# A one-layer encoder step: source order for the first stage on two engines, an earlier identity, and a shared rotation of eight PSUM banks

## The chip, the cores and the metric

The kernel runs on one core of one Trainium2 chip. A core has five engines with queues of their own: TensorE (PE in the profile, its weight loads PEld), VectorE (DVE), ScalarE (ACT), GpSimd (POOL) and SyncE (SP), which here only issues DMAs. Each engine serves its queue in order and waits on semaphores. The metric is the device time of one execution in microseconds, lower is better.

## The reference

One layer of a streaming encoder, for 256 rows of a new stream and 8 streams of 16 rows each: 384 rows in all, which share the weights.

```python
h    = rmsnorm(x, norm_mix_g)
proj = h @ w_in                      # conv gate pair | q | k | v | forget logits | gate A | gate B
u    = glu_in[..., :D_CONV] * sigmoid(glu_in[..., D_CONV:])
z    = layernorm(causal_dwconv(concat([conv_buf, u]), conv_dw_w, conv_dw_b), conv_ln_g, conv_ln_b)
a_out = (z * sigmoid(z)) @ conv_pw_out
q, k = rmsnorm(q, q_norm_g), rmsnorm(k, k_norm_g)
logf = log_sigmoid(f_logit + b_forget)
b_out = attn_fn(q, k, v, logf) @ w_att_out
x    = x + (sigmoid(gate_a) * a_out + sigmoid(gate_b) * b_out) @ w_out
h2   = rmsnorm(x, norm_ffn_g)
up   = h2 @ w_up                     # gate half | value half, each 5632 wide
gc   = causal_dwconv(concat([ffn_buf, g_half]), ffn_dw_w, ffn_dw_b)
x    = x + (silu(gc) * u_half) @ w_down
```

The model is 2048 wide, with 8 heads of 128. All is float32, and besides the rows the new k, v, logf and the two convolution states are returned.

## The kernel before, in words

Every product is made in three float32r matmuls. A weight block `raw` (256 rows by up to 512 columns, two k steps) is loaded from HBM, ScalarE casts it to `hi` (L145), and VectorE subtracts for `lo` (L146). The activations are kept as such pairs too, 16 chunks of 128 features. A unit is one k step of one job: three row tiles (or four feature tiles) times hi x hi, hi x lo, lo x hi, nine matmuls on L244 to L246, or twelve on L239 to L241 where the weights are the stationary side. A job accumulates 8 to 16 k steps in three PSUM banks (four on L239 to L241) and is then evacuated.

The order of the work is set in several ways. TensorE's order is the source's for the whole kernel (`pe_order`, a manual schedule). ScalarE, VectorE and SyncE are ordered by hand only in the opening part, up to the second weight block; after that a planner orders their instructions by readiness in its own model and by a priority. The priority is the place in the source, moved ahead by an offset: 150 for loads and splits (`SPLIT_AHEAD`), 400 for evacuations (`EVAC_AHEAD`). `queued` adds an edge to the engine's newest queued instruction, which fixes the order of the two and waits for nothing. `tc.keep_in_program_order` adds such an edge to the instruction before in the source. Before, `queued` is used on SP alone, for loads.

`plan` lists the weight blocks in the order of use, and `ahead(n)` loads and splits blocks until n are ready. In the first stage (the v columns, 344 wide, two jobs interleaved and then a third) n is 2, later 3. There are three raw, three hi and three lo tiles. `gemm` walks the units, and after each calls `tick`, which advances side work: generators that yield once per unit.

The side work of the first stage is `first_norm`: per chunk c of x, `x_chunk(c)` transposes three row tiles on TensorE (L285), copies them to hi, times the norm's gain, on ScalarE (L288) and makes lo on VectorE (L289). Chunks 2 and 3 are transposed after the third and fourth unit and used in the fifth and sixth; the block used there is the third. For each four chunks ScalarE makes three squares with a sum (L400). The sums give the row scale `rs1`, through a root on ScalarE and a Newton step on VectorE (`newton_rsqrt`, L110 to L116), which the evacuations of v need (`tok_evac`, L428).

The identity for transposes and for warm-up matmuls (L308) is made on POOL by a memset and a select. POOL's queue also issues the loads of eight small vectors (L348 to L352).

PSUM has eight banks in two pools: five `acc`, which the jobs take, and three `misc`, for transposes and the small products of attention. Only the second of two interleaved jobs takes its third bank from misc. The evacuation of k and q makes the squares for the head norm within the loop over the three banks (L431 to L434).

Attention is side work in the four convolution-gate jobs (L239 to L241): per head six steps at set units, with the loads of cached k and v on SP. The taps of the depthwise convolution (L722) run on VectorE beside it and after it. Behind attention come the gate jobs, the attention and convolution outputs (`ao_evac` L828, `pw_evac` L843 and L844, `mix_chunk` L850), the output product, and the feed-forward part, which ends in `down` jobs (L1018).

Of the kernel before, what the change touches and what calls it, by code (L numbers as in the profile page):

```python
# [8 lines left out]
F32 = mybir.dt.float32  # L9
F32R = mybir.dt.float32r  # L10
AF = mybir.ActivationFunctionType
ALU = mybir.AluOpType
# [3 lines left out]
P = 128  # L16
DM = 2048
NT = 384
NTT = 3
# [11 lines left out]
LN_LAG = 0  # L31
SQ_LAG = 1
MIX_FIRST, MIX_EVERY = 2, 2
SPLIT_AHEAD, EVAC_AHEAD = 150, 400

R_FFN, R_DWB, R_LNG, R_LNB, R_FDB, R_QG, R_N = 0, 16, 24, 32, 40, 84, 85
WARM, FILL = 5, 2
# [3 lines left out]
def hybrid_step(  # L41
# [34 lines left out]
    def f(ap):  # L76
        return ap.bitcast(F32)
# [39 lines left out]

    def rsqrt(m, shape, p, tag):
        s = p.tile(shape, F32, tag=tag + "s", name=tag + "s")
        r = p.tile(shape, F32, tag=tag + "r", name=tag + "r")  # L120
        newton_rsqrt(r[:], s[:], m)
        return r
# [19 lines left out]
        return [wp.tile([P, 2, 512], F32R, tag=tag, bufs=3, name=tag) for tag in ("hi", "lo")]  # L142

    def split_rows(hi, lo, raw, o, k):
        nc.scalar.copy(hi[:, k, :o], raw[:, k, :o])  # L145
        tt(lo[:, k, :o], raw[:, k, :o], f(hi[:, k, :o]), op=ALU.subtract)  # L146

    def split(raw, o):
        hi, lo = split_tiles()
# [56 lines left out]
    def grouped(tiles):  # L206
        def get(k):
            t = tiles[k // 4]
            return t[:, 0, k % 4, :], t[:, 1, k % 4, :]
        return get  # L210
# [7 lines left out]
        for g in sides:  # L218
            next(g, None)

    def gemm(jobs, sides=()):
        for js in jobs:
            js = js if isinstance(js, tuple) else (js,)
            for j in js:
                nb = 4 if j["kind"] == "A" else NTT
                j["ps"] = [(misc_tile if j is not js[0] and i == 2 else acc_tile)() for i in range(nb)]
            for j, k in [(j, k + i) for k in range(0, js[0]["nk"], 2) for j in js for i in range(2)]:
                nb, n, nk, ps = len(j["ps"]), j["n"], j["nk"], j["ps"]
                kk = k % 2
                if kk == 0:  # L230
                    ahead(2 if len(plan) > v_last + 3 else 3)
                    hi, lo = ready.pop(0)
                ah, al = j["act"](k)
                st, sp = k == 0, k == nk - 1
                for m in range(nb):
                    s = slice(m * P, (m + 1) * P)
                    if j["kind"] == "A":
                        o = ps[m][:, :NT]
                        mm(o, hi[:, kk, s], ah, start=st, stop=False)  # L239
                        mm(o, hi[:, kk, s], al, start=False, stop=False)  # L240
                        mm(o, lo[:, kk, s], ah, start=False, stop=sp)  # L241
                    else:
                        o = ps[m][:, :n]
                        mm(o, ah[:, s], hi[:, kk, :n], start=st, stop=False)  # L244
                        mm(o, ah[:, s], lo[:, kk, :n], start=False, stop=False)  # L245
                        mm(o, al[:, s], hi[:, kk, :n], start=False, stop=sp)  # L246
# [35 lines left out]
    def x_chunk(c):  # L282
        ps = misc_tile()
        for t in range(NTT):
            tr(ps[:, t * P:(t + 1) * P], xs[c // 4][:, t, c % 4 * P:(c % 4 + 1) * P], ident[:])  # L285
        g = gm[:, c:c + 1]
        hi, lo = hT[c // 4][:, 0, c % 4, :], hT[c // 4][:, 1, c % 4, :]
        nc.scalar.activation(hi, ps[:, :NT], AF.Identity, scale=g)  # L288
        stt(lo, ps[:, :NT], g, f(hi), op0=ALU.mult, op1=ALU.subtract)  # L289

    pe_order = tc.manual_schedule(engines={ENG.PE})
    pe_order.__enter__()
# [52 lines left out]
    rows = [(norm_ffn_g, R_FFN, 16), (conv_dw_b, R_DWB, 8), (conv_ln_g, R_LNG, 8),  # L345
            (conv_ln_b, R_LNB, 8), (ffn_dw_b, R_FDB, 44), (q_norm_g, R_QG, 1)]
    for v, r, n in rows:
        nc.gpsimd.dma_start(vrow[r:r + n, :], v[0].rearrange("(c p) -> c p", p=P))  # L348
    kg = p_qkv.tile([P, P], F32, name="kg")
    nc.gpsimd.dma_start(kg[:], k_norm_g[0].partition_broadcast(P))  # L350
    bf = p_qkv.tile([P, H], F32, name="bf")
    nc.gpsimd.dma_start(bf[:], b_forget[0].partition_broadcast(P))  # L352
# [35 lines left out]
    def first_norm():  # L388
        for c in range(2, 16, 2):
            if c == 2:  # L390
                yield
            yield
            x_chunk(c)
            yield
            x_chunk(c + 1)
            if c % 4 == 2:
                for t in range(NTT):
                    n = c // 4
                    tc.keep_in_program_order(
                        nc.scalar.activation(junk[:], xs[n][:, t, :], AF.Square, accum_out=ssx[:, t, n:n + 1]))  # L400
            yield
            if c > 2:
                yield
        mt = p_x0.tile([P, NTT], F32, name="mt")
        nc.vector.tensor_reduce(mt[:], ssx[:], axis=mybir.AxisListType.X, op=ALU.add)
        ts(mt[:], mt[:], 1.0 / DM, EPS, op0=ALU.mult, op1=ALU.add)
        r = rsqrt(mt[:], [P, NTT], p_x0, "r1")
        nc.vector.tensor_copy(rs1[:], r[:])
# [11 lines left out]
    lg = p_qkv.tile([P, NTT, H], F32, name="lg")  # L420
    ssq = p_qkv.tile([P, 2, NTT, H], F32, name="ssq")

    def tok_evac(dst, c0, n, sq=None, shared=True):
        def ev(t, ps):
            if shared and t % 2:
                ts(dst[:, t, c0:c0 + n], ps[:, :n], rs1[:, t:t + 1], None, op0=ALU.mult)
            else:
                nc.scalar.activation(dst[:, t, c0:c0 + n], ps[:, :n], AF.Identity, scale=rs1[:, t:t + 1])  # L428
            if sq is not None:
                for i in range(n // P):  # L430
                    jk = p_qkv.tile([P, P], F32, tag="jk", bufs=2, name="jk")  # L431
                    h = c0 // P + i
                    nc.scalar.activation(jk[:], dst[:, t, h * P:(h + 1) * P], AF.Square,
                                         accum_out=ssq[:, sq, t, h:h + 1])  # L434
        return ev

    ha = grouped(hT)
# [76 lines left out]
    gemm([job("B", 16, ha, tok_evac(kt, 512 * i, 512, 0)) for i in range(2)], [bias_rows()])  # L514
    close_b()
    rk = head_rsqrt(0)
    for t in range(NTT):
# [6 lines left out]
    gemm([job("B", 16, ha, tok_evac(qt, 512 * i, 512, 1)) for i in range(2)])  # L524
    rq = head_rsqrt(1)
    for t in range(NTT):
        q3 = qt[:, t, :].rearrange("p (h d) -> p h d", h=H)
# [123 lines left out]
    def attention():  # L651
        at = {}
        for d in heads:
            for off, step in ((0, head_past_keys), (2, head_operands), (4, head_scores), (9, head_probs),
                              (11, head_out), (13, head_last)):
                at[ATT_FIRST + 6 * d["h"] + off] = step, d
        for t in range(max(at) + 1):
            if t in at:
                step, d = at[t]
                step(d)  # L660
                if step is head_out and d["h"] + 2 < H:
                    load_v(d["h"] + 2)
            yield
# [104 lines left out]
    def sig_evac(dst, n):  # L768
        def ev(t, ps):
            nc.scalar.activation(cols_of(dst, t, n), ps[:], AF.Sigmoid, scale=rs1[:, t:t + 1])  # L770
        return ev
# [59 lines left out]
    def ao_job(n):  # L831
        return job("B", 8, grouped(aHL), ao_evac(n))

    gemm([ao_job(n) for _, n in AO_PW[:2]], [ln_steps])
    drain(ln_steps)


# [27 lines left out]
    def pw_done(n):  # L865
        def done():
# [5 lines left out]
        return done  # L872

    gemm([ao_job(n) if what == "ao" else job("B", 8, grouped(zt), pw_evac(n), done=pw_done(n))
          for what, n in AO_PW[2:]])


    res = {}
# [50 lines left out]
        r2 = rsqrt(m2[:], [P, NTT], p_f, "r2")  # L929
        nc.vector.tensor_copy(rs2[:], r2[:])  # L930

    gemm([job("B", 16, grouped(mix), wo_evac(n), done=wo_done(n)) for n in range(4)])


    p_f, y, xg, rs2, close_f, close_r = (res[k] for k in ("f", "y", "xg", "rs2", "close_f", "close_r"))
# [88 lines left out]
        return [job("B", 4 * len(gs), grouped(tiles), evac(n)) for n in range(4)]  # L1024

    for what, g in FFN_PLAN:
        gemm(up_jobs(g) if what == "up" else down_jobs(g, g[-1] == 10))

    pe_order.__exit__(None, None, None)
    close_f()  # L1030
# [42 lines left out]
```

## Time and profile before

| | |
|---|---|
| median of 3 runs | 2005.61 us (2002.94 to 2005.78) |
| profiled execution | 2005.83 us |
| its span, first to last instruction | 2003.9 us |
| instructions | 24493 |
| busy: DVE, ACT, POOL | 1272.2, 742.1, 87.2 us |
| HBM traffic over the span | 137 GB/s |

In the profile a row of the timeline is start, duration, engine, line, operation, output<-inputs, shapes, count, and in brackets the idle time before it with what ended it. Matmuls overlap in the pipeline, so the distance between starts is the pace and the duration is longer. The granted clock is TensorE's, as a share of full speed. A busy share close to 1 for TensorE says only that it always had a matmul in flight.

### The profile page before, as it was taken

The numbers are of one execution on the slowest core, as the hardware profiler recorded it, in microseconds if no ns is written. First come the engines' busy times: TensorE is split into PE (matmuls) and PEld (weight loads), VectorE is DVE, ScalarE is ACT, GpSimd is POOL, SyncE is SP. The second block draws the span as 40 slices with busy tenths as digits, with TensorE's granted clock in tenths as the row PEclk, the third lists the DMA queues.
The fourth block names the chain that finished last, engine by engine and source line by source line (L and its number), as shares of the span: only waits on it lengthen the run. The fifth ranks groups of instructions, "written<-read, shape, count | busy, mean of one in ns | idle before, by whom it ended". The sixth has DMA issues, their size and how long they took to land.

```text
span 2003.9 us, 24493 instructions
## 1 busy us (share of the span) xinstructions
PE 1992.6 (99%) x9431; PEld 1681.5 (84%) x9431; DVE 1272.2 (63%) x1852; ACT 742.1 (37%) x1077; POOL 87.2 (4%) x216
## 2 busy tenths in 40 slices
PE   8999999999999999999999999999999999999999
PEld 8988999988888887888888888888888888888887
DVE  4435478888765487676867683367673376638663
ACT  5434455433334523334433432233332233323321
POOL 2000001100000000000010000001000000000000
PEclk9999999999999999999999999999999999999999
DMA  6566566444444334534444444444443444344443
GB/s 179 176 175 175 137 163 167 120 140 131 132 134 125 127 121 142 185 121 133 127 137 116 137 127 137 126 127 126 129 135 127 133 120 137 126 129 125 137 157 106
DMA packets 209254, 275.99 MB, mean 138 GB/s; under 512 B 55878, under 2 KB 96729, under 8 KB 209129
## 3 DMA queue, kind: packets, MB, share of 16 engines
q1 hardware_dynamic: 208817, 273.85, 46.3%
q8 instruction: 74, 1.21, 0.2%
q0 software_dynamic: 288, 0.57, 0.2%
q14 instruction: 43, 0.35, 0.1%
q10 hardware_dynamic: 32, 0.01, 0.0%
HBM read 266.98 MB, written 7.86 MB: 137 GB/s over the span
## 4 chain that ended last, share of the span: by engine, by line
PE 95%; DVE 4%; issue 1%; DMA 1%; ACT 0%; SPq 0%; ACTq 0%; DVEq 0%
PE acc L244 28%; PE acc L246 28%; PE acc L245 28%; PE acc L239 2%; PE acc L241 2%; PE acc L240 2%; DVE mixT L259 1%; DVE lo L146 1%; DMA raw<-in_w_in_dram 1%; DVE sgA L843 0%; DVE uT L259 0%; DVE sgA L844 0%; PE misc L636 0%; PE misc L603 0%; PE misc L285 0%
## 5 line engine op out<-in xcount | busy, mean ns | idle before, releaser
L146 DVE TENSOR_TENSOR lo<-raw,hi 128x1024 fp32r<-128x1024 f32 (+2 forms) x481 | 579.6, 1205 | 582.7 <-ACT hi L145 579.0
L145 ACT CAST hi<-raw 128x1024 fp32r<-128x1024 f32 (+2 forms) x481 | 496.0, 1032 | 994.2 <-PE acc L246 869.1
L244 PE MATMUL acc<-hi,xg 128*128 128x512 f32 x1056 | 411.8, 390 | 0.0
L246 PE MATMUL acc<-hi,xg 128*128 128x512 f32 x1056 | 410.9, 389 | 0.0
L245 PE MATMUL acc<-lo,xg 128*128 128x512 f32 x1056 | 410.8, 389 | 0.0
L244 PE MATMUL acc<-hi,hT 128*128 128x512 f32 (+1 forms) x704 | 268.5, 381 | 2.4 <-ACT hT L288 2.4
L246 PE MATMUL acc<-hi,hT 128*128 128x512 f32 (+1 forms) x704 | 266.0, 378 | 0.4 <-DVE hT L289 0.4
L245 PE MATMUL acc<-lo,hT 128*128 128x512 f32 (+1 forms) x704 | 265.8, 377 | 0.0
L244 PEld LDWEIGHTS acc<-hi,xg 128*128 128x128 f32 x1056 | 198.2, 188 | 42.3
L246 PEld LDWEIGHTS acc<-hi,xg 128*128 128x128 f32 x1056 | 198.2, 188 | 41.3
L245 PEld LDWEIGHTS acc<-lo,xg 128*128 128x128 f32 x1056 | 198.2, 188 | 40.6
L244 PE MATMUL acc<-hi,act 128*128 128x512 f32 x528 | 205.5, 389 | 0.5 <-DVE y L1018 0.5
L246 PE MATMUL acc<-hi,act 128*128 128x512 f32 x528 | 205.4, 389 | 0.0
L245 PE MATMUL acc<-lo,act 128*128 128x512 f32 x528 | 205.4, 389 | 0.0
L722 DVE SCALAR_TENSOR_TENSOR ut<-ext,cw,ut 128x384 f32<-128x384 f32 x240 | 151.5, 631 | 6.1
L244 PEld LDWEIGHTS acc<-hi,hT 128*128 128x128 f32 x704 | 132.7, 189 | 25.3 <-ACT hT L288 2.7
L246 PEld LDWEIGHTS acc<-hi,hT 128*128 128x128 f32 x704 | 132.7, 189 | 23.3 <-DVE hT L289 0.7
L245 PEld LDWEIGHTS acc<-lo,hT 128*128 128x128 f32 x704 | 132.8, 189 | 22.2
L259 DVE STREAM_TRANSPOSE extf<-tok 32x384 f32<-32x384 f32 x176 | 100.3, 570 | 30.9 <-ACT tok L954 28.2
L259 DVE STREAM_TRANSPOSE uT<-tok 32x384 f32<-32x384 f32 x176 | 100.3, 570 | 29.7 <-ACT tok L954 26.9
L244 PEld LDWEIGHTS acc<-hi,act 128*128 128x128 f32 x528 | 99.1, 188 | 21.6 <-DVE y L1018 0.9
L245 PEld LDWEIGHTS acc<-lo,act 128*128 128x128 f32 x528 | 99.1, 188 | 20.5
(289 smaller groups left out, 2079.7 us busy)
## 6 DMA issues: line engine op xcount, KB each, us to landing
raw<-in_w_up_dram SPq DMA_DIRECT2D x176, 512.0 KB
raw<-in_w_in_dram SPq DMA_DIRECT2D x96, 512.0 KB
raw<-in_w_down_dram SPq DMA_DIRECT2D x88, 512.0 KB
raw<-in_w_in_dram SPq DMA_DIRECT2D x64, 256.0 KB
raw<-in_w_out_dram SPq DMA_DIRECT2D x32, 512.0 KB
raw<-in_w_att_out_dram SPq DMA_DIRECT2D x16, 512.0 KB
raw<-in_conv_pw_out_dram SPq DMA_DIRECT2D x16, 512.0 KB
raw<-in_w_in_dram SPq DMA_DIRECT2D x23, 344.0 KB
```

The lines of the kernel that those rows point to most:

```text
L145: nc.scalar.copy(hi[:, k, :o], raw[:, k, :o])
L146: tt(lo[:, k, :o], raw[:, k, :o], f(hi[:, k, :o]), op=ALU.subtract)
L239: mm(o, hi[:, kk, s], ah, start=st, stop=False)
L240: mm(o, hi[:, kk, s], al, start=False, stop=False)
L241: mm(o, lo[:, kk, s], ah, start=False, stop=sp)
L244: mm(o, ah[:, s], hi[:, kk, :n], start=st, stop=False)
L245: mm(o, ah[:, s], lo[:, kk, :n], start=False, stop=False)
L246: mm(o, al[:, s], hi[:, kk, :n], start=False, stop=sp)
L259: nc.vector.transpose(put(a, slice(32 * b, 32 * b + 32)), src[32 * a:32 * a + 32, b])
L722: stt(o, v, wc, o, op0=ALU.mult, op1=ALU.add)
```

## The change

It has these parts:

- In the first stage (`in_first`: from the start until four blocks of the third v job are fetched) the casts and splits of weight blocks, all x copies, the last three squares, the root and ScalarE's v evacuations are chained in source order, each on its engine. The x copies also get the evacuations' priority. The last squares, the mean and `rs1` come without the two ticks between them, and the 14 ticks until the small columns keep the place of those.
- The identity's select is chained on POOL ahead of the vector loads, which are chained too.
- The squares of k and q are made after all three evacuations of a job.
- Attention steps get a priority offset of 250.
- With `wide=True`, in all jobs behind attention, each job takes two acc banks and one misc bank.

```diff
-SPLIT_AHEAD, EVAC_AHEAD = 150, 400
+SPLIT_AHEAD, ATT_AHEAD, EVAC_AHEAD = 150, 250, 400
...
-    make_identity(nc, ident[:])
+    nc.gpsimd.memset(ident[:], 0.0)
+    queued(nc.gpsimd.affine_select(out=ident[:], in_=ident[:], pattern=[[-1, P]], compare_op=ALU.not_equal, fill=1.0,
+                                   base=0, channel_multiplier=1))
...
-        nc.scalar.activation(s, m, AF.Sqrt)
+        queued(nc.scalar.activation(s, m, AF.Sqrt), in_first())
...
     def split_rows(hi, lo, raw, o, k):
-        nc.scalar.copy(hi[:, k, :o], raw[:, k, :o])
-        tt(lo[:, k, :o], raw[:, k, :o], f(hi[:, k, :o]), op=ALU.subtract)
+        first = in_first()
+        queued(nc.scalar.copy(hi[:, k, :o], raw[:, k, :o]), first)
+        queued(tt(lo[:, k, :o], raw[:, k, :o], f(hi[:, k, :o]), op=ALU.subtract), first)
...
+    def in_first():
+        return len(plan) >= v_last - 4
...
-    def gemm(jobs, sides=()):
+    def gemm(jobs, sides=(), wide=False):
...
-                j["ps"] = [(misc_tile if j is not js[0] and i == 2 else acc_tile)() for i in range(nb)]
+                j["ps"] = [(misc_tile if i == 2 and (wide or j is not js[0]) else acc_tile)() for i in range(nb)]
...
+                    if "post" in j:
+                        j["post"]()
...
-        nc.scalar.activation(hi, ps[:, :NT], AF.Identity, scale=g)
-        stt(lo, ps[:, :NT], g, f(hi), op0=ALU.mult, op1=ALU.subtract)
+        with tc.high_priority(offset=EVAC_AHEAD):
+            queued(nc.scalar.activation(hi, ps[:, :NT], AF.Identity, scale=g))
+            queued(stt(lo, ps[:, :NT], g, f(hi), op0=ALU.mult, op1=ALU.subtract))
...
-        nc.gpsimd.dma_start(vrow[r:r + n, :], v[0].rearrange("(c p) -> c p", p=P))
+        queued(nc.gpsimd.dma_start(vrow[r:r + n, :], v[0].rearrange("(c p) -> c p", p=P)))
...
+                    if c == 14:
+                        queued(sq)
+                    else:
+                        tc.keep_in_program_order(sq)
...
-        for _ in range(12):
+        for _ in range(14):
...
+        d["post"] = post
...
-                nc.scalar.activation(dst[:, t, c0:c0 + n], ps[:, :n], AF.Identity, scale=rs1[:, t:t + 1])
+                queued(nc.scalar.activation(dst[:, t, c0:c0 + n], ps[:, :n], AF.Identity, scale=rs1[:, t:t + 1]),
+                       in_first())
...
-                step(d)
+                with tc.high_priority(offset=ATT_AHEAD):
+                    step(d)
...
-    gemm([job("B", 16, ha, sig_evac(sg, n)) for sg in (sgA, sgB) for n in range(4)], [ln_steps])
+    gemm([job("B", 16, ha, sig_evac(sg, n)) for sg in (sgA, sgB) for n in range(4)], [ln_steps], wide=True)
```

The last edit, `wide=True`, stands the same way in the four other calls of `gemm` behind attention: the two of the outputs, the output product, and the feed-forward part.

More of the change, by code (lines that the diff above doesn't have):

```diff
@@ L347, in hybrid_step @@
     for v, r, n in rows:
-        nc.gpsimd.dma_start(vrow[r:r + n, :], v[0].rearrange("(c p) -> c p", p=P))
+        queued(nc.gpsimd.dma_start(vrow[r:r + n, :], v[0].rearrange("(c p) -> c p", p=P)))
     kg = p_qkv.tile([P, P], F32, name="kg")
-    nc.gpsimd.dma_start(kg[:], k_norm_g[0].partition_broadcast(P))
+    queued(nc.gpsimd.dma_start(kg[:], k_norm_g[0].partition_broadcast(P)))
     bf = p_qkv.tile([P, H], F32, name="bf")
-    nc.gpsimd.dma_start(bf[:], b_forget[0].partition_broadcast(P))
+    queued(nc.gpsimd.dma_start(bf[:], b_forget[0].partition_broadcast(P)))
     ones = cp.tile([P, P], F32, name="ones")
@@ L398, in first_norm @@
                     n = c // 4
[L399 to L402, printed above, removed]
+                    sq = nc.scalar.activation(junk[:], xs[n][:, t, :], AF.Square, accum_out=ssx[:, t, n:n + 1])
+                    if c == 14:
+                        queued(sq)
+                    else:
+                        tc.keep_in_program_order(sq)
+            if c < 14:
+                yield
+            if 2 < c < 14:
                 yield
         mt = p_x0.tile([P, NTT], F32, name="mt")
[L405 to L408, printed above, removed]
-        for _ in range(12):
+        with tc.high_priority(offset=EVAC_AHEAD):
+            nc.vector.tensor_reduce(mt[:], ssx[:], axis=mybir.AxisListType.X, op=ALU.add)
+            ts(mt[:], mt[:], 1.0 / DM, EPS, op0=ALU.mult, op1=ALU.add)
+            r = rsqrt(mt[:], [P, NTT], p_x0, "r1")
+            nc.vector.tensor_copy(rs1[:], r[:])
+        for _ in range(14):
             yield
@@ L421, in hybrid_step, with tok_job, post, tok_evac @@
     ssq = p_qkv.tile([P, 2, NTT, H], F32, name="ssq")
-    def tok_evac(dst, c0, n, sq=None, shared=True):
+    def tok_job(dst, c0, n, sq):
+        d = job("B", 16, ha, tok_evac(dst, c0, n))
+        def post():
+            for t in range(NTT):
+                for h in range(c0 // P, (c0 + n) // P):
+                    jk = p_qkv.tile([P, P], F32, tag="jk", bufs=2, name="jk")
+                    nc.scalar.activation(jk[:], dst[:, t, h * P:(h + 1) * P], AF.Square,
+                                         accum_out=ssq[:, sq, t, h:h + 1])
+        d["post"] = post
+        return d
+    def tok_evac(dst, c0, n, shared=True):
         def ev(t, ps):
@@ L427, in ev @@
             else:
-                nc.scalar.activation(dst[:, t, c0:c0 + n], ps[:, :n], AF.Identity, scale=rs1[:, t:t + 1])
[L429 to L434, printed above, removed]
+                queued(nc.scalar.activation(dst[:, t, c0:c0 + n], ps[:, :n], AF.Identity, scale=rs1[:, t:t + 1]),
+                       in_first())
         return ev
@@ L512, in head_rsqrt @@
         return rsqrt(ssf, [P, NTT * H], p_qkv, f"rq{a}")[:].rearrange("p (t h) -> p t h", t=NTT)
-    gemm([job("B", 16, ha, tok_evac(kt, 512 * i, 512, 0)) for i in range(2)], [bias_rows()])
+    gemm([tok_job(kt, 512 * i, 512, 0) for i in range(2)], [bias_rows()])
     close_b()
@@ L522, in hybrid_step @@
     nc.sync.dma_start(sample_k[0].rearrange("b t h d -> (b t) (h d)"), kt[:, 2, :])
-    gemm([job("B", 16, ha, tok_evac(qt, 512 * i, 512, 1)) for i in range(2)])
+    gemm([tok_job(qt, 512 * i, 512, 1) for i in range(2)])
     rq = head_rsqrt(1)
@@ L832, in ao_job @@
         return job("B", 8, grouped(aHL), ao_evac(n))
-    gemm([ao_job(n) for _, n in AO_PW[:2]], [ln_steps])
+    gemm([ao_job(n) for _, n in AO_PW[:2]], [ln_steps], wide=True)
     drain(ln_steps)
@@ L874, in hybrid_step @@
     gemm([ao_job(n) if what == "ao" else job("B", 8, grouped(zt), pw_evac(n), done=pw_done(n))
-          for what, n in AO_PW[2:]])
+          for what, n in AO_PW[2:]], wide=True)
     res = {}
@@ L930, in second_norm @@
         nc.vector.tensor_copy(rs2[:], r2[:])
-    gemm([job("B", 16, grouped(mix), wo_evac(n), done=wo_done(n)) for n in range(4)])
+    gemm([job("B", 16, grouped(mix), wo_evac(n), done=wo_done(n)) for n in range(4)], wide=True)
     p_f, y, xg, rs2, close_f, close_r = (res[k] for k in ("f", "y", "xg", "rs2", "close_f", "close_r"))
@@ L1026, in hybrid_step @@
     for what, g in FFN_PLAN:
-        gemm(up_jobs(g) if what == "up" else down_jobs(g, g[-1] == 10))
+        gemm(up_jobs(g) if what == "up" else down_jobs(g, g[-1] == 10), wide=True)
     pe_order.__exit__(None, None, None)
```

## The prediction

> **What bounds the kernel now.** I read the spans and the page first, then the waits of TensorE, then the first 22 us instruction by instruction, then the places behind attention where TensorE waits for a bank.
>
> ```profile
> core 0: 2003.9 us, clock 0.999
> ```
> ```profile
> PE 1992.6 (99%) x9431; PEld 1681.5 (84%) x9431; DVE 1272.2 (63%) x1852; ACT 742.1 (37%) x1077; POOL 87.2 (4%) x216
> ```
>
> TensorE is busy for 1992.6 of 2003.9 us, and its instruction order is fixed by hand and untouched by the change. Nothing that shortens DVE or ACT work in itself counts; only TensorE's own waits do, and the stretch in which its clock is not at full speed. The waits view of TensorE, columns total, times, longest:
>
> ```profile
> PE acc L244 <- ACT hT L288: 2.4, 1, 2.4
> PE acc L244 <- DVE y L1018: 0.5, 1, 0.5
> PE acc L246 <- DVE hT L289: 0.4, 1, 0.4
> PE acc L244 <- DVE sgB L828: 0.4, 2, 0.2
> PE misc L850 <- DVE sgA L844: 0.2, 1, 0.2
> PE acc L244 <- DVE sgA L843: 0.2, 1, 0.2
> ```
>
> The first and third are the x copies of chunk 2 at the start; y, sgB and sgA L843 are evacuations that hold a bank; L850 waits for data. The attention lines do not appear at all. So the ceiling is small: a few us out of 2005.83, the profiled execution's own time, which is 0.22 us over the median of the runs shown (2005.61). All sums below are against 2005.83; the 1.9 us around the span stays.
>
> Windows over three clock periods (us, PE busy (x), granted clock, DMA share, GB/s):
>
> ```profile
> 10.62:14.04 3.42, 3.17 (x22) 1.00 0.96 325
> 14.04:17.45 3.41, 0.84 (x3) 1.00 0.73 229
> 17.45:20.86 3.41, 3.41 (x13) 0.50 0.89 265
> ```
>
> TensorE was busy for only 0.84 us of 14.04 to 17.45, and the whole next period ran at clock 0.50. So the hole is paid twice: once as waiting, and 3.41 x 0.5 = 1.7 us again as slow matmuls.
>
> **The start, step by step.** ACT, then DVE, then TensorE of the same stretch:
>
> ```profile
> 12.85 0.77 ACT L145 CAST hi<-raw 128x688 fp32r<-128x688 f32 x1 [3.96 <-DMA raw<-in_w_in_dram]
> 14.94 0.77 ACT L145 CAST hi<-raw 128x688 fp32r<-128x688 f32 x1 [1.32 <-DMA raw<-in_w_in_dram]
> 15.61 0.57 ACT L288 ACTIVATE hT<-misc,gm 128x384 fp32r<-128x384 f32 x1
> 16.08 0.76 ACT L145 CAST hi<-raw 128x688 fp32r<-128x688 f32 x1
> 16.74 0.58 ACT L288 ACTIVATE hT<-misc,gm 128x384 fp32r<-128x384 f32 x1
> 17.21 0.63 ACT L400 ACTIVATE junk<-xs 128x512 f32<-128x512 f32 x1
> ```
> ```profile
> 13.65 0.87 DVE L146 TENSOR_TENSOR lo<-raw,hi 128x688 fp32r<-128x688 f32 x1 [3.76 <-ACT hi L145]
> 15.73 0.88 DVE L146 TENSOR_TENSOR lo<-raw,hi 128x688 fp32r<-128x688 f32 x1 [1.21 <-ACT hi L145]
> 16.53 0.61 DVE L289 SCALAR_TENSOR_TENSOR hT<-misc,gm,hT 128x384 fp32r<-128x384 f32 x1
> ```
> ```profile
> 11.56 0.49 PE L285 MATMUL misc<-ident,xs 128*128 128x128 f32 x3
> ```
> ```profile
> 13.30 0.49 PE L285 MATMUL misc<-ident,xs 128*128 128x128 f32 x3
> 16.23 0.43 PE L244 MATMUL acc<-hi,hT 128*128 128x344 f32 x1 [2.44 <-ACT hT L288]
> 16.50 0.32 PE L245 MATMUL acc<-lo,hT 128*128 128x344 f32 x1
> 17.19 0.45 PE L246 MATMUL acc<-hi,hT 128*128 128x344 f32 x1 [0.38 <-DVE hT L289]
> ...
> 21.20 0.32 PE L246 MATMUL acc<-hi,hT 128*128 128x344 f32 x1
> 21.36 0.49 PE L285 MATMUL misc<-ident,xs 128*128 128x128 f32 x3
> 21.60 0.41 PE L244 MATMUL acc<-hi,hT 128*128 128x344 f32 x1
> ```
>
> TensorE had transposed x chunk 2 by 12.05 and chunk 3 by 13.79. ACT casts the third weight block at 12.85, as soon as it has landed, and is free at 13.62. But next in its queue stands the cast of the fourth block, which lands only at 14.94; the copy of chunk 2, whose input has lain ready since 12.05, stands behind it. TensorE needs that copy for its next unit, and the fourth block only two units later. The order is upside down, and the source has it right: the block fetched at unit 4 is traced after both copies (ticks 2 and 3).
>
> With the chain, ACT does: cast 12.85 to 13.62, copy of chunk 2 to 14.19 (0.57), of chunk 3 to 14.77 (0.58), then the fourth cast at 14.94 as now. DVE does: lo of the third block 13.65 to 14.52 as now, lo of chunk 2 to 15.13 (0.61), of chunk 3 to 15.74, lo of the fourth block to 16.62, against 16.61 now, so the raw tile goes back to the loads no later. TensorE's first matmul of the unit can go at 14.2, the second at 14.5 (lo of the weights), the third at 15.15 (lo of x). The other six of this unit and the nine of the next follow at 0.16 (from 21.20 to 21.36): 16 x 0.16 = 2.56, so the transposes of chunk 4 start at 17.7 instead of 21.36. **Gain 3.65 us**, of which 1.7 is the clock; I take 3.6 for the hand-overs. What is late next is the third block itself (12.85, its DMA at 0.96 share), which nothing here moves.
>
> Does TensorE keep the 3.6? A set of transposes delays the next unit by 0.24 (21.36 to 21.60), and a unit is 9 x 0.16 = 1.44. The fourth block's lo at 16.62 is needed at 17.9. The fifth cast now stands behind the copy of chunk 4: transposes over at 18.2 (0.49), copy to 18.8, cast (0.76) to 19.5, lo (0.88) to 20.4; it is needed after two units and another set of transposes, at 21.1. That is 0.6 us to spare. Later in the stage the worst case repeats every four units: a cast behind a copy that itself waits for transposes ends, with its lo, 0.49 + 0.58 + 0.77 + 0.88 = 2.7 us after the unit before them; it is needed after two sets of transposes and two units, 2 x 0.24 + 2 x 1.44 = 3.4. Again 0.6 to spare. So the stage becomes tight but should not stall, and after it TensorE alone sets the pace.
>
> The last squares (0.63 each, with a read behind them) are now in the chain, the mean and root follow without the two ticks of before, with priority. ACT holds later casts behind them, but three blocks are prepared ahead by then. No wait stands at this place in the waits view, so bringing it forward gains nothing, and I cost it at nothing; if its cover were gone, the three squares, 3 x 0.63 = 1.9 us, would be the bound.
>
> **Identity.** POOL's order now:
>
> ```profile
> 1.39 0.68 POOL L348 DMA_DIRECT2D vrow<-in_norm_ffn_g_dram  x1 [0.37 <-issue]
> 2.15 0.32 POOL masks.py:199 TENSOR_SCALAR_AFFINE_SELECT ident<-ident 128x128 f32<-128x128 f32 x1
> ```
>
> The select moves ahead of that issue: 2.15 - 1.39 = 0.76 us sooner, and the warm-up with it. The first units then start a little earlier and wait for the third block at 12.85 all the same: gain 0, up to 0.76 if that cover were not there. The vector loads come 0.3 later each and are used in the second half of the stage: cost 0.
>
> **Banks behind attention.** The first wait of each kind:
>
> ```profile
> 721.59 0.39 PE L246 MATMUL acc<-hi,zt 128*128 128x512 f32 x1
> 722.16 0.50 PE L244 MATMUL acc<-hi,zt 128*128 128x512 f32 x1 [0.18 <-DVE sgB L828]
> 722.50 0.40 PE L245 MATMUL acc<-lo,zt 128*128 128x512 f32 x1
> ```
> ```profile
> 1721.80 0.39 PE L246 MATMUL acc<-hi,act 128*128 128x512 f32 x1
> 1722.67 0.50 PE L244 MATMUL acc<-hi,act 128*128 128x512 f32 x1 [0.48 <-DVE y L1018]
> 1723.01 0.39 PE L245 MATMUL acc<-lo,act 128*128 128x512 f32 x1
> ```
>
> A job takes three of five banks, so its third bank is the first of the job before, and DVE's late evacuation of that stops TensorE. With two acc banks and one misc bank a job finds its banks free a job earlier. Starts are 0.23 apart undisturbed: 0.57 + 0.34 - 0.46 = 0.45 for each of the two sgB waits, 0.87 + 0.34 - 0.46 = 0.75 for y. Sum 0.9 + 0.75 = 1.65. The sgA L843 wait goes too, but 3 us behind it TensorE waits at L850 for the data of that same evacuation, and would wait there by as much more: 0. **Gain 1.65 us**, bounds 0 (each wait reappears at the next use of DVE's result) and 2.1 (the third one counts as well).
>
> [...]
>
> **The rest.** The squares of k and q come after all three evacuations: no wait on a k or q evacuation stands in the waits view, so 0, and later than now by at most the evacuations between. The attention steps get priority over the splits (250 against 150): no wait to remove, so 0 or a loss, priced below.
>
> Sum: 2005.83 - 3.6 - 1.65 = 2000.6 us. Its own range is 1998.8 (identity's 0.76 and the third bank wait's 0.45 count too, and 0.6 of the 1.4 us that is left of the hole) to 2001.8 (most of the bank term lost).
>
> **Rivals.**
> The clock still falls. The hole shrinks from 2.8 us (2.44 and 0.38) to about 1.4 between 13.8 and 15.15, with the early units' head start 0.4 more. A period with 0.84 of 3.41 busy lost the clock; one with 3.17 kept it; the worst period would have about 1.6. In between nothing is measured. Price 1.7: 2002.3. Chance 0.16.
> [...]
>
> The bank waits only move on, as L850 does: 2000.6 + 1.65 = 2002.3. Against: the waits view shows a data wait behind only one of them. Chance 0.08.
>
> The squares of the first three groups, which are not chained, land in front of a cast that has 0.6 to spare: 1.9 - 0.6 = 1.3, three times: up to 2004.5. Against: casts have priority over them. Chance 0.09.
>
> The order does not change where it matters, or the fourth cast still goes first: 2005.8. Chance 0.05.
>
> Slower: attention steps jump in front of waiting casts and splits. In the eighth pass of the attention stage it is close already:
>
> ```profile
> 357.45 2.94 ACT L145 CAST hi<-raw 128x1024 fp32r<-128x1024 f32 x3
> ```
> ```profile
> 358.54 3.50 DVE L146 TENSOR_TENSOR lo<-raw,hi 128x1024 fp32r<-128x1024 f32 x3 [0.21 <-ACT hi L145]
> ```
> ```profile
> 360.54 0.44 PE L239 MATMUL acc<-hT,hi 128*128 128x384 f32 x1
> ```
>
> Three casts were held up, and the first lo ended at 358.54 + 1.17 = 359.71 for use at 360.54: 0.8 us to spare. If each of eight heads pushes its block back by one more cast and lo (0.98 + 1.17 = 2.15), TensorE waits 1.35 x 8 = 10.8: 2011.4. It cancels the gain from 0.8 + 5.25 / 8 = 1.5 us of push per head on. For it: both engines serve the queue in order, and an early attention step blocks it until TensorE's transposes. Against: TensorE waits for nothing in the whole stage now. Chance 0.10.
>
> **Numbers.** The forecast has 0.52. A measurement of this kernel can tell about 0.2%, 4.0 us, from no change: faster is below 2001.6, slower above 2009.6. Faster 0.50 (the forecast without the top of its range), slower 0.10, within 0.2% the remaining 0.40. The range runs from 1998.8 to 2005.8 and leaves out the slower rival and a little below.
>
> **What would show it.** Right: on ACT, the copies of chunks 2 and 3 before the fourth cast; chunk 4's transposes near 17.7; clock 1.00 in every period from 10.62 on; no TensorE wait on the sgB and y evacuations (L828 and L1018 now), and a longer one at the chunk transposes behind sgA. Wrong: a period at 0.50 still there; TensorE waits on hi or lo between 20 and 60 us or between 210 and 390; the third block landing at another time than 12.85, which sets the whole start.

## The result, and the profile after

The changed kernel is slower: 2024.82 us median (2023.93 to 2025.8, 5 executions) against 2005.61 for the kernel before (2002.94 to 2005.85, 5 executions), a ratio of 1.0098 with the interval 1.0087 to 1.0109. The forecast was 2000.6, range 1998.8 to 2005.8. The profiled execution took 2025.8 us, 19.97 us more than that of before. In what follows the ratios leave out two executions far above all others of their kernel: 2589.05 us of the kernel before beside f1 and g1, and 11530.44 us of e8.

TensorE's waits (total, times, longest). Line numbers are the changed kernel's from here on; rows of an experiment have that kernel's own. L293 and L297 are the x transposes and copies (L285 and L288 before), L571 the key loads (L550), L578 the first bias-row load (L557), L592 the transpose of cached keys (L571), L630 the softmax's reader of the scores (L609), L653 and L730 transposes and products that take a misc bank:

```profile
PE misc L730 <- DVE mx L630: 14.7, 1, 14.7
PE misc L653 <- DVE mx L630: 6.5, 1, 6.5
PE misc L317 <- POOL ident L109: 1.5, 1, 1.5
PE misc L872 <- DVE sgA L866: 0.5, 2, 0.3
```

The waits of before on hT, y, sgB and the sgA bank are gone, and the one at the chunk transposes behind sgA (now L872) is longer, as forecast. Two new waits, 21.2 us in all, both on the same reader, were in none of the views of before.

The start went as worked out. ACT of the changed kernel, then TensorE's transposes of x chunk 4, then the windows of the start and of the first new wait (PE busy (x), PEld, DVE, ACT, POOL, granted clock, DMA share, GB/s):

```profile
12.37 0.77 ACT L148 CAST hi<-raw 128x688 fp32r<-128x688 f32 x1 [3.86 <-DMA raw<-in_w_in_dram]
13.04 1.17 ACT L297 ACTIVATE hT<-misc,gm 128x384 fp32r<-128x384 f32 x2
14.45 0.77 ACT L148 CAST hi<-raw 128x688 fp32r<-128x688 f32 x1 [0.25 <-DMA raw<-in_w_in_dram]
```
```profile
17.26 0.49 PE L293 MATMUL misc<-ident,xs 128*128 128x128 f32 x3
```
```profile
14.04:17.45 3.41, 3.31 (x20) 3.00 (x20) 1.93 (x4) 3.00 (x8) 0.00 (x0) 1.00 0.79 226
17.45:20.86 3.41, 3.41 (x25) 3.39 (x24) 2.17 (x4) 2.47 (x4) 0.00 (x0) 1.00 0.66 206
...
270.20:273.65 3.45, 0.00 (x0) 0.00 (x0) 3.41 (x3) 0.00 (x0) 0.00 (x0) 1.00 0.38 60
273.65:277.06 3.41, 0.00 (x0) 0.00 (x0) 0.00 (x0) 0.00 (x0) 0.00 (x0) 0.50 1.31 211
...
287.30:290.72 3.42, 3.42 (x26) 2.78 (x24) 2.82 (x6) 1.05 (x3) 0.42 (x1) 0.50 0.28 68
290.72:294.13 3.41, 3.41 (x23) 3.41 (x23) 3.20 (x7) 0.57 (x1) 0.84 (x2) 1.00 0.82 169
```
```profile
273.65:290.72 17.07, 5.97 (x33) 5.27 (x33) 5.73 (x19) 3.09 (x11) 2.28 (x4) 0.50 0.72 173
345.33:352.16 6.83, 3.93 (x27) 3.29 (x28) 6.69 (x24) 2.83 (x9) 0.00 (x0) 0.50 0.46 131
```

Both copies stand ahead of the fourth cast, chunk 4 is transposed at 17.26 instead of 21.36, and the half-speed period at 17.45 is gone. But a wait of 14.7 us leaves TensorE idle through whole clock periods: the first of them still has 1.00, the next 0.50, and full speed returns only after one period of full work (287.30 to 290.72). The two half-speed stretches hold 5.97 + 3.93 = 9.90 us of matmuls, of which half, 4.95, is taken as extra. That is an estimate from the granted 0.50; the starts of the 128x384 matmuls lay 0.32 us apart in the first of these stretches (286.52 to 288.44) and 0.17 after it (291.97 to 293.88), which would make it 4.5. So attention lost about 21.2 + 4.95 = 26.15 us. Less 4.1 at the start (21.36 to 17.26) and 1.65 for the banks that leaves 20.4, against 19.97 measured.

Where does the wait come from? First TensorE and DVE of the changed kernel:

```profile
269.41 0.64 PE L624 MATMUL misc<-kTs,qz 128*32 128x128 f32 x16
284.75 0.48 PE L730 MATMUL misc<-ident,ut 128*128 128x128 f32 x1 [14.69 <-DVE mx L630]
```
```profile
270.12 1.25 DVE L592 STREAM_TRANSPOSE kTs<-kc 128x1024 f32<-128x1024 f32 x1 [3.31 <-PE misc L624]
...
284.39 0.29 DVE L630 CUSTOM_DVE_ANT_0 pr<-misc,bs 128x128 f32<-128x128 f32 x1 [10.79 <-POOL bs L584]
```

The scores are ready by about 270 in three misc banks. Their reader on DVE also needs the bias rows `bs`, and waits 10.79 us for POOL's addition to them. TensorE meanwhile wants a misc bank for L730 and has none. Now POOL, and SP, which issues the loads; first the changed kernel:

```profile
283.64 0.72 POOL L584 TENSOR_TENSOR bs<-bs,mk 128x256 f32<-128x256 f32 x1 [29.95 <-DMA bs<-c_dr]
```
```profile
239.92 2.51 SPq L571 DMA_DIRECT2D kc<-in_cache_k_dram  x4
244.24 4.50 SPq L139 DMA_DIRECT2D raw<-in_w_in_dram  x3
254.64 2.34 SPq L571 DMA_DIRECT2D kc<-in_cache_k_dram  x4
257.03 4.42 SPq L139 DMA_DIRECT2D raw<-in_w_in_dram  x4
271.39 2.23 SPq L571 DMA_DIRECT2D kc<-in_cache_k_dram  x4
273.67 1.70 SPq L139 DMA_DIRECT2D raw<-in_w_in_dram  x3
...
275.98 0.53 SPq L578 DMA_DIRECT2D bs<-c_dr  x1
```
```profile
SPq L571 <- DVE kTs L592: 10.5, 2, 9.9
```

The same head's rows in the kernel before, on SP, POOL and DVE:

```profile
243.51 0.41 SPq L557 DMA_DIRECT2D bs<-c_dr  x1
```
```profile
249.19 0.73 POOL L563 TENSOR_TENSOR bs<-bs,mk 128x256 f32<-128x256 f32 x1 [103.88 <-DMA bs<-c_dr]
```
```profile
273.12 0.29 DVE L609 CUSTOM_DVE_ANT_0 pr<-misc,bs 128x128 f32<-128x128 f32 x1 [2.16 <-PE misc L595]
```

This is the third of the eight heads (number 2, counted from 0). `load_k` for the next head is called inside an attention step (`head_past_keys`) and so took the new priority with it; `load_v`, which also loads the bias rows, is called outside. Before, head 2's bias rows go to SP at 243.51, ahead of head 3's keys (245.62), and are added 24 us before their reader at 273.12. After, three key sets, those of heads 3, 4 and 5, and ten weight fetches stand ahead of head 2's bias rows. Each set needs a `kc` tile, which an earlier head's transpose L592 frees. The third set's is freed at 271.37, because that transpose writes the one `kTs` tile, which head 2's own score products (L624 at 269.41) still read. So SP stands still for 9.9 us, to 271.39: head 2's bias rows wait behind a load that waits for head 2's scores. They are issued at 275.98, 32.5 us later than before; POOL adds at 283.64, and the scores are read at 284.39 instead of 273.12.

### The profile page after: what moved, and what is told of

It is laid out like the page before. It is cut to its first block, busy times and chain, and to the rows that moved or that the text cites. A ratio compares the mean times of both kernels' runs of the same rounds, so it can differ in the third digit from the quotient of the medians.

```text
span 2023.8 us, 24482 instructions
## 1 busy us (share of the span) xinstructions
PE 1995.7 (99%) x9431; PEld 1684.5 (83%) x9431; DVE 1274.4 (63%) x1852; ACT 742.7 (37%) x1077; POOL 85.7 (4%) x216
## 4 chain that ended last, share of the span: by engine, by line
PE 96%; DVE 2%; DMA 1%; SPq 1%; issue 0%; ACT 0%; POOL 0%; DVEq 0%; ACTq 0%
PE acc L250 20%; PE acc L252 20%; PE acc L251 20%; PE misc L250 9%; PE misc L252 9%; PE misc L251 9%; PE acc L245 2%; PE acc L246 2%; PE acc L247 2%; DVE lo L149 0%; DVE mixT L267 0%; DVE ut L744 0%; DMA raw<-in_w_in_dram 0%; PE misc L657 0%; DMA bs<-c_dr 0%
## 5 line engine op out<-in xcount | busy, mean ns | idle before, releaser
L250 PE MATMUL acc<-hi,xg 128*128 128x512 f32 x704 | 274.9, 390 | 0.0
L252 PE MATMUL acc<-hi,xg 128*128 128x512 f32 x704 | 273.9, 389 | 0.0
L251 PE MATMUL acc<-lo,xg 128*128 128x512 f32 x704 | 273.9, 389 | 0.0
L250 PE MATMUL acc<-hi,hT 128*128 128x512 f32 (+1 forms) x576 | 218.3, 379 | 0.1
L252 PE MATMUL acc<-hi,hT 128*128 128x512 f32 (+1 forms) x576 | 215.7, 374 | 0.1
L251 PE MATMUL acc<-lo,hT 128*128 128x512 f32 (+1 forms) x576 | 215.5, 374 | 0.0
L250 PEld LDWEIGHTS acc<-hi,xg 128*128 128x128 f32 x704 | 132.1, 188 | 28.4
L252 PEld LDWEIGHTS acc<-hi,xg 128*128 128x128 f32 x704 | 132.1, 188 | 27.6
L251 PEld LDWEIGHTS acc<-lo,xg 128*128 128x128 f32 x704 | 132.2, 188 | 27.0
L252 PE MATMUL misc<-hi,xg 128*128 128x512 f32 x352 | 137.0, 389 | 0.0
L250 PE MATMUL misc<-hi,xg 128*128 128x512 f32 x352 | 137.0, 389 | 0.0
L251 PE MATMUL misc<-lo,xg 128*128 128x512 f32 x352 | 136.9, 389 | 0.0
L250 PE MATMUL acc<-hi,act 128*128 128x512 f32 x352 | 136.9, 389 | 0.0
L251 PE MATMUL acc<-lo,act 128*128 128x512 f32 x352 | 136.9, 389 | 0.0
L252 PE MATMUL acc<-hi,act 128*128 128x512 f32 x352 | 136.9, 389 | 0.0
```

## The experiments

Theory A: the whole loss is that key loads moved ahead of bias rows on SP. Theory B: the attention steps' own DVE and ACT work, placed ahead of splits and casts, does it. Theory C: the faster first stage makes attention come too early for its loads. Of the kernels from e2 to e7 there is one execution each, of those of e1, e8, f1 and g1 7 to 11.

**e1: no priority for the attention steps.** The rest of the change stays.

```diff
-                with tc.high_priority(offset=ATT_AHEAD):
-                    step(d)
+                step(d)
```

> The changed kernel with one part undone: the attention steps have no priority of their own again. Theory A (the priority moves the loads of cached keys ahead of the loads of the bias rows in SP's queue, the bias rows land late, and the scores that wait for them hold the misc banks) and theory B (the priority moves the steps' own DVE and ACT work ahead of the splits) both expect the two waits of 14.7 and 6.5 us and the two half-clock stretches to go: about 2000 us (2025.8 less the 25.8 us by which the attention stage is longer than before). Theory C (the earlier first stage makes attention reach its data too early) expects most of the 20 us to stay: above 2015 us.

Measured: 2000.51 us median (1999.07 to 2001.01), ratio to before 0.9975 (0.9966 to 0.9985). Its largest wait but the identity's:

```profile
PE acc L250 <- ACT hT L297: 0.8, 1, 0.8
```

The loss is the priority's and no other part's; C falls. What is left has the time that the prediction gave to the whole, 2000.6.

**e2: the priority alone**, on the kernel before.

```diff
-                step(d)
+                with tc.high_priority(offset=ATT_AHEAD):
+                    step(d)
```

> The kernel before with only the priority of the attention steps. Theories A and B expect about 2030 us (2005.8 and the 25.8 us of the attention stage), with the same two waits on the scores' reader. Theory C expects about 2006 us.

Measured: 2027.75 us. The same two waits at the same places, without the first stage's order and without the banks:

```profile
PE misc L709 <- DVE mx L609: 13.6, 1, 13.6
PE misc L632 <- DVE mx L609: 6.5, 1, 6.5
```

**e3: key loads without the priority.** All of the change, but `load_k` is called outside the priority's block.

```diff
-        if d["h"] + 1 < H:
-            load_k(d["h"] + 1)
...
+                if step is head_past_keys and d["h"] + 1 < H:
+                    load_k(d["h"] + 1)
```

> The changed kernel, with the load of the next head's cached keys taken out of the step, so that it has no priority, as the load of values and bias rows has none. The steps keep theirs. Theory A expects about 2000 us and no wait of TensorE on the scores' reader. Theory B expects 2015 us or more, since the DVE and ACT work still goes first.

Measured: 2009.01 us, so 15.8 of the 24.3 us between the changed kernel and e1 are gone, and the wait of 14.7 with them. Two waits on the scores' reader are left, at 342 and 361, 5.0 us in all, the later of 3.6. SP and then DVE of this kernel at the later one:

```profile
344.50 12.11 SPq L139 DMA_DIRECT2D raw<-in_w_in_dram  x6
...
357.23 0.52 SPq L578 DMA_DIRECT2D bs<-c_dr  x1
```
```profile
364.62 0.29 DVE L628 CUSTOM_DVE_ANT_0 pr<-misc,bs 128x128 f32<-128x128 f32 x1 [4.71 <-POOL bs L584]
```

Bias rows late again, this time of the last head and behind six weight fetches that wait for raw tiles. In the kernel before the same rows also stood behind six fetches, but went out at 347.02, 10 us sooner (e1: 343.9). So the steps' priority delays loads that do not have it themselves; by which link was not followed.

**e4: bias rows and values get the priority too.**

```diff
-                if step is head_out and d["h"] + 2 < H:
-                    load_v(d["h"] + 2)
+                    if step is head_out and d["h"] + 2 < H:
+                        load_v(d["h"] + 2)
```

> The changed kernel, with the load of values and bias rows given the same priority as the steps, so that both kinds of load move alike. Theory A expects about 2000 us, since the bias rows are issued ahead of the key loads that wait for a tile. Theory B expects 2015 us or more.

Measured: 2029.1 us: A's number was missed, and B's was met. The largest of TensorE's waits, then of SP's on these loads:

```profile
PE acc L245 <- ACT hi L148: 13.2, 4, 4.4
PE acc L247 <- DVE lo L149: 4.2, 4, 1.8
```
```profile
SPq L576 <- PE misc L657: 30.4, 6, 9.1
```

No wait on the scores' reader is left. Now the value loads (L576) stand ahead of the weight fetches and wait, six times and 30.4 us, for a tile that the attention output (L657) still reads. So A was too narrow: it is not only the order of keys and bias rows; here a value load that waited for a tile, up to 9.1 us, held the loads behind it, as a key load did for 9.9 us in the changed kernel. But what TensorE waits for here is not the weights' landing. SP, ACT and a window (its last three: granted clock, DMA share, GB/s) at the first of the four places, where TensorE stands from 270.69 to 274.88:

```profile
262.24 4.44 SPq L139 DMA_DIRECT2D raw<-in_w_in_dram  x6
```
```profile
269.76 0.40 ACT L633 ACTIVATE pr<-pr,mx 128x128 f32<-128x128 f32 x1 [2.49 <-DVE mx L632]
...
273.80 2.92 ACT L148 CAST hi<-raw 128x1024 fp32r<-128x1024 f32 x3
```
```profile
271.00:272.00 1.00, 0.00 (x0) 0.00 (x0) 1.00 (x2) 0.54 (x3) 0.00 (x0) 1.00 0.00 0
```

The transfers of the six fetches are over before 271, but ACT makes the exponentials first and casts at 273.80. At the three other places, too, the transfers are over before TensorE's wait on `hi` begins, and the casts come behind exponentials. That is B's mechanism, and here it costs 17.4 us of waits and the clock that goes with them (0.993 in the mean, against 1.000 in e1).

**e5: key loads first, alone.** The version without the steps' priority (e1), and the priority on `load_k` only.

```diff
-            load_k(d["h"] + 1)
+            with tc.high_priority(offset=ATT_AHEAD):
+                load_k(d["h"] + 1)
```

> The changed kernel without the priority of the steps, but with that priority on the load of the next head's cached keys alone. Theory A in its first form (the key loads' priority over the bias loads is the cause) expects 2020 us or more. Theory A in a narrower form (what counts is whether the bias rows of head 2 are issued behind key loads that wait for a tile of a later head) expects about 2000 to 2003 us, because here SP's order has the bias rows of head 2 behind the second set of key loads and not behind the third. Theory B expects about 2000 us.

Measured: 2014.18 us, between the theories' numbers. Bias rows were issued in time here (259.29 for head 2), and yet their reader made TensorE wait, 2.7 us at one place and 5.4 at three others. DVE:

```profile
270.69 1.25 DVE L592 STREAM_TRANSPOSE kTs<-kc 128x1024 f32<-128x1024 f32 x1 [3.31 <-PE misc L625]
271.86 1.18 DVE L149 TENSOR_TENSOR lo<-raw,hi 128x1024 fp32r<-128x1024 f32 x1
272.96 0.28 DVE L631 CUSTOM_DVE_ANT_0 pr<-misc,bs 128x128 f32<-128x128 f32 x1
```

With the keys there earlier, the planner puts the next head's key transpose and a split ahead of the reader on DVE, 1.25 + 1.18 us in which the banks stay held. This is a second cost of early key loads; it explains 2.7 us at this place, not the 14.7 of the changed kernel; the three other places were not followed.

**e6: bias rows from POOL's queue.** All of the change, priority included; the four loads of `bs` per head are issued by POOL.

```diff
-        nc.sync.dma_start(bs[:, 0:P], c_dr[h, 0:P].partition_broadcast(P))
+        nc.gpsimd.dma_start(bs[:, 0:P], c_dr[h, 0:P].partition_broadcast(P))
```

> The changed kernel with the priority as it is, but with the four loads of the bias rows issued by POOL instead of SP, so that no key load stands ahead of them. Both forms of theory A expect the waits of TensorE on the scores' reader to go: 2000 to 2006 us, the upper end if POOL's own issue is slower. Theory B expects 2015 us or more, since the DVE and ACT work has the same priority as before.

Measured: 2008.56 us, between the two theories' numbers. All waits on the scores' reader are gone, and one of 6.2 us on a cast (`hi`) is new. ACT at that place:

```profile
305.57 0.39 ACT L726 COPY ext<-ut 128x240 f32<-128x240 f32 x1 [4.16 <-DVE ut L744]
...
307.54 0.40 ACT L633 ACTIVATE pr<-pr,mx 128x128 f32<-128x128 f32 x1
...
309.65 1.03 ACT L148 CAST hi<-raw 128x1024 fp32r<-128x1024 f32 x1
```

Here ACT waits 4.16 us for a convolution step of DVE and then makes the exponentials, before the cast that TensorE waits for: B's mechanism again, at one place, with 6.2 us of wait; the granted clock of this execution is 0.998 in the mean, against 1.000 in e1.

**e7: key loads from POOL's queue.** The other way round: the bias rows stay on SP, the keys go.

```diff
-            nc.sync.dma_start(kc[q, :].rearrange("k (b j d) -> k b j d", b=8, j=4),
+            nc.gpsimd.dma_start(kc[q, :].rearrange("k (b j d) -> k b j d", b=8, j=4),
```

> The kernel after, with the four loads of cached keys per head issued by POOL, so that on SP nothing of the attention steps stands in front of the bias rows or the weight fetches; the priority of the steps stays. If the whole loss sits on SP's queue (theory A): no TensorE wait on the scores' reader or on hi and lo, 1999 to 2002 us. If the steps' own exponentials and copies also hold up casts on ACT (theory B, which the wait of 6.2 us on hi in the kernel with bias loads on POOL suggests): waits of TensorE on hi or lo of some us come back, each with a clock period at half speed, 2004 to 2010 us. If POOL's bias additions are held up behind key loads that wait for their tile: waits on the scores' reader as after, above 2015 us.

Measured: 2000.45 us, the time of e1, with the priority of the steps fully in place. Its largest wait but the identity's is 0.6 us, on a split. POOL and DVE for head 2:

```profile
256.44 1.74 POOL L584 TENSOR_TENSOR bs<-bs,mk 128x256 f32<-128x256 f32 x1
```
```profile
269.46 0.29 DVE L630 CUSTOM_DVE_ANT_0 pr<-misc,bs 128x128 f32<-128x128 f32 x1 [2.15 <-PE misc L616]
```

The reader now waits for nothing but TensorE's own scores; the bias rows were added 11 us before (256.44 to 258.18, then 269.46). So the loss needs the key loads on SP. The priority of the steps' DVE and ACT work over the splits cost nothing that can be seen in this execution; in e4 and e6, where loads with the priority wait on SP, it did, though how the waiting loads bring about that order on ACT is in no view. The same transfers from another engine took 24.4 us off here (2024.82 to 2000.45): what was saved is not the issue (0.4 to 0.6 us each on SP in the rows above) but the issuing engine's wait, up to 9.9 us, for the tile to come free, with the other loads behind it.

**f1 and g1: the two good parts, each alone** on the kernel before: all edits of the first stage without the identity and the `wide` calls; and the `wide` calls without the rest. The edits are those of the change.

> The kernel before with the order of the first stage alone (chained casts, splits, x copies, last squares, root and v evacuations; no identity, no banks, no attention priority, k and q squares as before). The prediction's step expects a gain of 3.6 us (1.7 of it clock): about 2002 us against 2005.6. If the hole and the half-clock stretch are only in some executions of the kernel before, as in the run with the priority alone, where TensorE waited 0.8 and 0.4 us there and the clock stayed at 1.00, the median gain is smaller: 2 us.

> The kernel before with the rotation of eight banks behind attention alone. The prediction's step expects a gain of 1.65 us: about 2004 us against 2005.6, no wait on the evacuations of sgB and y, and a longer one at the chunk transposes behind sgA. The rival (the waits only move on) expects no difference.

Measured: 2002.16 us for the first stage, ratio 0.9987 (0.9977 to 0.9996), against 2005.46 beside it, 3.3 us; 2003.61 for the banks, ratio 0.9991 (0.9982 to 0.9999), 1.85 us. Together 5.15; e1 has 4.9. The banks' waits go as forecast, and the data wait behind sgA takes 0.5 in g1 instead of 0.2.

**e8: e1 with the chunk transposes behind sgA one unit later.**

```diff
-MIX_FIRST, MIX_EVERY = 2, 2
+MIX_FIRST, MIX_EVERY = 3, 2
```

> The version without the priority of the attention steps, with the chunk transposes behind sgA one unit later (MIX_FIRST 3 for 2), so that the evacuation they read has 1.4 us more. Expected by the sum of waits: its two waits of 0.5 us in all go, 0.5 us less than that version's 2000.51 us, 1999.5 to 2000.5; if the wait only moves to the next reader of the bank, no change.

Measured: 1999.46 us median of 7, ratio 0.9969 (0.9958 to 0.9981), the fastest here. The wait on sgA is gone from its waits, and that on hT was 0.2 in this execution instead of 0.8. It lies 1.05 us below e1, but the two intervals overlap, so only the wait's going is shown, not the whole difference.

## Why the prediction was wrong, and where it was right

- **The step that failed** is the last one before the sum: "The attention steps get priority over the splits (250 against 150): no wait to remove, so 0 or a loss", taken at 0 with 2005.83 - 3.6 - 1.65. It measured 24.3 us in medians (2024.82 against e1) and 25.05 between the two profiled executions (2025.8 and 2000.75). The rows give 25.35: two waits of 14.7 and 6.5 us and the estimated 4.95 us of half clock, less a wait of 0.8 at the start that e1's execution has and the other has not. What was overlooked is what a step issues besides its ACT and DVE work: four key loads on SP. Of those the text said nothing, though the timeline of SP before shows them between weight fetches and bias rows.
- **The slower rival** (2011.4, chance 0.10) had the right part of the change and the wrong queue. It priced one more cast and lo per head, 1.35 us each, on ACT and DVE. e7 keeps exactly that priority on ACT and DVE and loses nothing, and the changed kernel has no wait on a cast or split at all, so this mechanism is refuted as the cause of the loss. It is a real one all the same: it stood once in e6, with 6.2 us, and four times in e4, with 17.4.
- "Against: TensorE waits for nothing in the whole stage now" was no argument: it says that nothing is late, not how little would make it late. The bias rows had 24 us to spare at head 2 and by head 7 only 5 (added at 356.98, read at 361.95), and the key loads that the change moves on SP go past them. A price of the half-speed clock was set only for the start; the waits of 6.5 and 14.7 us in attention brought it too (clock 0.50 from 345.33 to 352.16 and from 273.65 to 290.72).
- **First stage**: 3.65 forecast, 4.1 in the profile (chunk 4 at 17.26), 3.3 in the medians of f1. The order on ACT, the time and the clock came as worked out; the third block landed 0.5 earlier in this execution (cast at 12.37, not 12.85), which is luck and makes up the difference. The rivals on the clock and on the squares did not come: the squares ran from 15.13 to 17.35, behind the fourth cast.
- **Banks**: 1.65 forecast, 1.85 by g1. The rival that the waits only move on is refuted: only that at sgA did, 0.2 to 0.5, as the text said.
- **Identity, squares of k and q**: costed at nothing, not run alone. TensorE's warm-up waits 1.5 for it instead of 2.5 (e1 against f1). With both left in, e1 came out at 2000.51 against the forecast 2000.6, so close in part by luck: the first stage alone gave less than its term and the banks more.
- **Still open**: how the planner comes to the order of the second place. There, at head 5, the bias rows were added by 340.56, and the scores done a little before, but DVE had a key transpose, nine taps and a split ahead of the reader, which ran at 347.88. The wait of 6.5 us is in e2 and not in e6 or e7, which have key loads and bias rows on two engines; e3 has 1.4 us at this place. So it goes with both kinds of load on SP, but the link from them to that order is in no view.

## What to carry to other kernels

When the priority of a step is raised, list all that it issues, its DMAs first, and for each load ask which tile must come free and what stands behind it on that engine's queue: an early load that waited for a tile stopped the later ones here, for 9.9 us in the changed kernel. Look for a chain that leads back to the same step: here the bias rows of a head stood behind a load that waited until the scores of that head were computed, and the scores then waited for the bias rows. And try the parts of a bundle alone: two of them gained 5 us together while one lost 24.

## What the runs showed of the hardware

The clock fell after periods that were not wholly idle (0.84 us of matmuls in the kernel before, 1.37 in e4), and in g1 it stayed at 1.00 through the start hole. In the changed kernel its changes at 273.65, 290.72, 345.33 and 352.16 lie 5, 16 and 2 steps of 3.413 us apart, and the next one, at 2021.27, 489 steps further on. The grid of these periods lay elsewhere in other profiled executions. In the profile of before its edges are at 14.04, 17.45 and 20.86; in that of g1 the clock falls at 1998.44, and counted back from there in the same steps, an estimate, the edges are at 11.89, 15.30 and 18.71. So the start hole of before lies in one period, which holds 0.84 us of matmuls, and that of g1, somewhat shorter (waits of 1.9 and 0.4 us, not 2.4 and 0.4), in two. The windows of g1, then four of e4, columns as above:

```profile
11.89:15.30 3.41, 2.49 (x18) 2.21 (x16) 0.88 (x1) 1.06 (x2) 0.00 (x0) 1.00 0.95 325
15.30:18.71 3.41, 2.03 (x11) 1.75 (x12) 2.71 (x4) 3.38 (x8) 0.00 (x0) 1.00 0.71 209
18.71:22.12 3.41, 3.41 (x25) 3.37 (x24) 1.22 (x2) 2.02 (x5) 0.00 (x0) 1.00 0.79 254
```
```profile
269.32:272.73 3.41, 1.37 (x21) 0.74 (x20) 3.27 (x14) 2.26 (x9) 0.00 (x0) 1.00 0.12 42
272.73:276.15 3.42, 1.01 (x2) 0.50 (x2) 3.28 (x7) 3.19 (x6) 0.00 (x0) 0.50 0.65 96
...
341.00:344.41 3.41, 1.58 (x23) 1.14 (x21) 3.41 (x13) 1.39 (x5) 0.00 (x0) 1.00 0.01 4
344.41:347.83 3.42, 0.62 (x2) 0.30 (x2) 3.35 (x9) 2.87 (x6) 0.00 (x0) 1.00 0.26 72
```

A period with 1.37 us of matmuls was followed by half speed, one with 1.58 was not. The prediction had nothing between 0.84 and 3.17. In the traces of the kernel before and of the changed kernel, from 10 us to the last matmul, the full-speed periods that half speed followed held 0.84 us in the one and 0.00, 0.00 and 1.42 us in the other (the last at 2017.86 to 2021.27); all other full-speed periods held 2.13 us or more, and full speed followed them. Between 1.42 and 1.58 nothing was measured here. So the start hole cost clock in the profiled execution of before and none in that of g1, where it was 0.5 us shorter and lay across an edge of the grid. Within one period it would have left 0.84 + 0.5 = 1.34 us there, less than 1.37 and 1.42; by this estimate it was the place in the grid that saved the clock.

The start hole of the kernel before cost its 1.7 us of clock (3.41 x 0.5, an estimate) in the profiled execution; whether it does in every one was not shown. Beside f1 and g1 six of its executions lay between 2003.05 and 2003.99 us and fourteen between 2005.07 and 2007.31. That the two groups are those without and with the half-speed period is likely, from their distance of about 2 us, but only the profiled executions show the period itself.
